# Laying plain row blocks between the four steps of a seven-product pair, in an encoder layer

## The chip, the core and the metric

The kernel runs on one core of a Trainium2 chip. The metric is the device time of one execution in microseconds; where several runs are shown, their median counts. Beside the runs there is one profiled execution, from which every view below is taken. A core has five engines that work at the same time and wait for one another by semaphores: TensorE (PE in the profile; its weight loads are PEld), VectorE (DVE), ScalarE (ACT), GpSimd (POOL) and SyncE (SP), whose queue issues most of the DMAs here.

## The reference, cut to what matters

One encoder layer over 256 tokens of width 4096, all in float32:

```python
h = rms_norm(x, g_mix)
proj = h @ w_in            # q latent, kv latent, rotary key, gate a | q_b, k_b, v_b, gate b
y_a = rms_norm(mla(...)) * silu(gate_a)
y_b = rms_norm(dilated(q_b, k_b, v_b)) * silu(gate_b)
x = x + concat(y_a, y_b) @ w_out
x = x + (p @ w_ple) * sigmoid(rms_norm(x, g_ple) @ w_ple_gate)
return rms_norm(x, g_final)
```

Nearly all of the arithmetic is in the three large products: with w_in (4096 x 11840), w_out and w_ple_gate (4096 x 4096 each).

## The kernel before, in words

**Products.** Every float32 operand is split into a high half (the value rounded to a shorter float, made by ScalarE: `split`, L115) and a low half (the rest, by VectorE: L116). A product of two tiles is then three matmuls into the same PSUM bank: high by high (L133), low weight by high (L134), high weight by low (L135). "Low" of L134 is that of the streamed weights, so L134 is the first matmul that needs VectorE's part of a conversion. The names of the tiles are `raw` for what a DMA brings, `hi` and `lo` for the halves; when a conversion goes to another place in memory, the name of that place stands instead (`B`, `T`, `Ah`, `Al` and so on).

**Row blocks.** The reduction over 4096 runs over 32 row blocks of 128. A load (L793) brings 128 rows of 1024 columns of the weights, 512 KB, into one of four `raw` tiles (`RAW = 4`). The 256 tokens are two halves of 128, the 1024 columns two halves of 512, so a row block that is done plainly takes four products (`plain_step`, one step).

**Seven-product blocks.** A block (`class Block`, L763 on) is 1024 output columns over all 32 row blocks. Some row blocks are taken in pairs: 2x2 halves of tokens and rows against 2x2 halves of rows and columns, done with seven products in place of eight. Such a pair is four steps (`fast_steps`), here called s1 to s4:

- s1 loads both row blocks; VectorE makes two differences (T[0]) and the low half of one half-width tile; 1 product
- s2 converts the second row block (high half L830, low half L833), and VectorE makes two more differences (T[1]; all differences are recorded at L817); 2 products
- s3 converts T[0], s4 converts T[1]; 2 products each

The differences and sums on the side of the tokens are made once, ahead of the block, by `add_sums`. T has one buffer. After the last step of the last pair a task forms the middle sums (`gates_mid`, `d_mid` with L669 and L672, `out_mid` with L904, `wide_mid`), which frees four of the eight PSUM banks; after the last step of the block another adds the rest (`d_done` with L687, `out_done` with L924 and the transposes of L730, `wide_done`).

There are 13 such blocks, 86 pairs in all: ga (part of gate a); q0, k0, v0, q1, k1, v1 (the dilated branch); three of w_out (called o0 to o2 here) and three of w_ple_gate. The rest of the columns goes through plain steps of two row blocks by 512 columns (`Old`).

**Order.** The program is written out by hand. `steps` is the list of all steps, and PE runs them in this order. How a block's pairs and plain row blocks follow one another was a string: in "CCSCSC..." a C is two plain steps and an S the four steps of a pair (`mix`, L1155; `lay`, L1161). k0, v0, q1 and k1 have "CSCSCSCSCSCSCSSC", eight pairs of which the last two stand back to back; the w_out block o1 and two of w_ple_gate end in "SSCC" and "SSCeC" (e: two steps with w_ple).

**Rings.** The converted tiles of a step lie in a ring: three `wp` tiles, and, in a block, further places that are idle at that time (`ring`). The main loop converts up to five steps ahead of the step that PE gets next, three more than otherwise (two), if the step's ring has more than three places; `tiles` gives no tile while its last user hasn't run (in the order of the program). All conversions stand in the in-order queues of ScalarE and VectorE together with the tasks above, in the order in which the program emits them. In k1 the last four letters (`spare = 4`) had the three `wp` tiles alone, because their fourth place, B4, becomes the result's.

Of the kernel before, what the change touches and what calls it, by code (L numbers as in the profile page):

```python
# [15 lines left out]
ALU = mybir.AluOpType  # L16
# [3 lines left out]
S = 256  # L20
# [58 lines left out]
def encoder_layer(ctx: ExitStack, tc: tile.TileContext, x, p, positions, g_mix, w_in, g_q_latent, w_uq,  # L79
                  g_kv_latent, w_ukv, g_out_mla, g_out_dil, w_out, w_ple, g_ple, w_ple_gate, g_final,  # L80
                  c_inv, c_dist, out):
    nc = tc.nc
    x, p, out = x[0], p[0, 0], out[0]
    w_in, w_uq, w_ukv, w_out, w_ple, w_ple_gate = (w[0] for w in (w_in, w_uq, w_ukv, w_out, w_ple, w_ple_gate))
# [24 lines left out]
    def plain(t):  # L109
        return t.bitcast(F32)  # L110
# [194 lines left out]
    T7 = {}  # L305

    sums = stat(NT * 6).rearrange("p (c t) -> p c t", t=NT)
# [162 lines left out]
    pairs = {}  # L470
# [182 lines left out]
    def d_mid(key, blk):  # L653
        def task():
            tags = D_TAGS[key]
            if len(tags) == 2:
                d = [slot(b, [NT, 512]) for b in tags]
            else:
                both = slot(tags[0], [2, NT, 512])
                d = [both[:, 0], both[:, 1]]  # L660
            D[key] = d
            if key == ("v", 1):
                E["d"] = slot("T5", [2, NT, S])
                nc.gpsimd.dma_start(E["d"], c_dist)
            ps = blk.ps
            sc = [(rxq if key[0] == "q" else rx)[:, t:t + 1] for t in range(NT)]

            def add(h, t, m, old):
                nc.vector.scalar_tensor_tensor(d[h][:, t], ps[m], sc[t], old, op0=ALU.mult, op1=ALU.add)  # L669

            for t in range(NT):
                nc.scalar.activation(d[0][:, t], ps["M1"], AF.Copy, scale=sc[t])  # L672
            for t in range(NT):
                add(1, t, "M6", d[0][:, t])
            add(0, 1, "M7", d[1][:, 1])
            add(1, 0, "M5", d[1][:, 0])
            add(1, 1, "M5", d[0][:, 1])
            flags.add(("mid", key))
            yield
        return task  # L680
# [71 lines left out]
    WP = ["wp"] * 3  # L752

    class Step:
# [4 lines left out]
        def __init__(self, load, split, run, needs=(), frees=0):  # L759
            self.load, self.split, self.run, self.needs, self.frees, self.after = load, split, run, needs, frees, None  # L760
            self.ring = WP
# [3 lines left out]
    class Block:  # L765
# [6 lines left out]

        NAMES = "M2", "X", "M3", "M4", "M1", "M5", "M6", "M7"

        def __init__(self, w, lhs, sums, name, order, needs, tags, tmp, ring, spare=0):
            self.w, self.lhs, self.sums, self.name, self.needs, self.tmp = w, lhs, sums, name, needs, tmp
            self.spare = spare
            self.ring, self.tags = ring, dict(zip(self.NAMES, tags))
            self.ps, self.left = {}, {}
            for kind, _ in order:  # L780
                for m in ("M1", "M5", "M7", "M6", "M4", "M2", "M3") if kind == "fast" else ("M2", "X", "M3", "M4"):
                    self.left[m] = self.left.get(m, 0) + (1 if kind == "fast" else 2)

        def product(self, m, a, b):
            first = m not in self.ps
# [23 lines left out]
        def fast_steps(self, j):  # L809

            r, T = [], []
            (A11, A21), (A12, A22) = [[lambda k=k, t=t: tuple(q[:, t * P:(t + 1) * P] for q in self.lhs(k))
                                       for t in range(NT)] for k in (2 * j, 2 * j + 1)]
            S = lambda n: (lambda: self.sums[j][n])

            def sub(dst, a, b):
                nc.vector.tensor_tensor(dst, a, b, op=ALU.subtract)  # L817

            def split1(hi, lo):
                if isinstance(self.tmp, tuple):  # L820
                    T.extend(slot(b, [2, Q]) for b in self.tmp)
                else:
                    both = slot(self.tmp, [4, Q])
                    T.extend((both[:, :2], both[:, 2:]))
                sub(T[0][:, 0], r[0][:, 1], r[0][:, 0])
                sub(T[0][:, 1], r[0][:, 1], r[1][:, 1])
                split(hi[:, 0], lo[:, 0], r[0][:, 0])

            def split2(hi, lo):
                nc.scalar.activation(hi, r[1], AF.Copy)  # L830
                sub(T[1][:, 0], r[1][:, 1], T[0][:, 0])
                sub(T[1][:, 1], r[1][:, 0], T[1][:, 0])
                nc.vector.tensor_tensor(lo, r[1], plain(hi), op=ALU.subtract)  # L833

            def run(*which):
                def go(hi, lo):
                    for i, (m, a) in enumerate(which):
                        self.product(m, a(), (hi[:, i], lo[:, i]))
                return go

            needs = [*self.needs(2 * j), *self.needs(2 * j + 1), (self.name, j)]
            return [
                Step(tuple(lambda k=k: r.append(self.load(k)) for k in (2 * j, 2 * j + 1)), split1, run(("M1", A11)), needs, 1),
                Step(None, split2, run(("M2", A12), ("M3", S(3))), needs, 1),
                Step(None, lambda hi, lo: split(hi, lo, T[0]), run(("M5", S(0)), ("M7", S(2))), needs, 0),
                Step(None, lambda hi, lo: split(hi, lo, T[1]), run(("M6", S(1)), ("M4", A22)), needs, 0),
            ]
# [304 lines left out]
    EVEN, ODD = ("m0", "m1", "s", "o", "m2", "m3", "t0", "t1"), ("m2", "m3", "t0", "t1", "m0", "m1", "s", "o")  # L1152
    LAST = "m2", "m3", "s", "o", "m0", "m1", "t0", "t1"

    def mix(shape, pairs=range(16)):  # L1155

        chosen = list(pairs)[:shape.count("S")]
        fast, plain_ = iter(chosen), iter(j for j in range(16) if j not in chosen)
        return [("ple", 0) if x == "e" else ("fast", next(fast)) if x == "S" else ("plain", next(plain_)) for x in shape]

    def lay(blk, order, mid, done, ple=None):  # L1161
        last = max(i for i, o in enumerate(order) if o[0] == "fast")
        for i, (kind, j) in enumerate(order):
            if kind == "fast":
                new = blk.fast_steps(j)
            elif kind == "ple":
                new = ple
            else:
                new = [x for kt in (2 * j, 2 * j + 1) for x in blk.plain_step(kt)]
            if i == last:  # L1170
                new[-1].after = mid
            if i == len(order) - 1:
                new[-1].after = done
            for x in new:
                x.ring = blk.ring if i < len(order) - blk.spare else WP
            steps.extend(new)

    def hook(at, f):
        assert at not in hooks
# [19 lines left out]

    hook(24, lambda: spawn(add_sums(7, x_pair, z0_dst, ("T2", "T3"), "x0_sums", x0_s, 2)))  # L1200
    gated_rings = {("T4", "T7"): ("mid", ("k", 1)), "Al1": ("y_sums", FAST_O - 1), ("T5", "T6"): "kpe"}
    order = mix("CCSCSCSCSCSCSCSC")
    blk = Block(w_in[:, OFF_GA:OFF_GA + 1024], lhs_x, x0_s, "x0_sums", order, lambda kt: (), LAST, ("T2", "T3"),
                WP + [("T5", "T6")])
    lay(blk, order, gates_mid(blk), gates_done(blk))
# [13 lines left out]
    x_s = {}  # L1219
# [10 lines left out]

    for n, key in enumerate((key, i) for i in range(2) for key in "qkv"):
        off = {"q": OFF_Q, "k": OFF_K, "v": OFF_V}[key[0]] + 1024 * key[1]
        full = "CSCSCSCSCSCSCSSC"
        order = mix("CCCCCCCCSCSCSCSC") if n == 0 else mix(full) if n < 5 else mix("CCCCSCSCSCSCSCSC", (0, 1, 2, 3, 6, 7))
        ring = (["B6"], ["B4", "B6"], ["B4", "B6"], ["B4"], ["B4"], [("T4", "T7")])[n]
        tags = LAST if n == 0 else ("t0", "t1", "m2", "m3", "m0", "m1", "s", "o") if n == 1 else (EVEN, ODD)[n % 2]
        blk = Block(w_in[:, off:off + 1024], lhs_x, x_s, "x_sums", order, lambda kt: (), tags, "B1", WP + ring,
                    4 if n == 4 else 0)
        lay(blk, order, d_mid(key, blk), d_done(key, blk))
    beside = [len(steps), len(steps) + 64]  # L1240
    for c in range(4):
        if c == 3:
# [5 lines left out]
    for k in range(WIDE_O):  # L1248
        hook(len(steps), only(*(("t0", "t1"), ("m0", "m1"), ("m2", "m3"))[k]))
        for h in range(2):  # L1250
            hook(len(steps) + 4 + h, lambda c=2 * k + h: load_res(c))
        order = mix(("CCCCCCSCSCSCSCCC", "CCSCSCSCSCSCSSCC", "CCCSCSCSCSCSCSCC")[k])
        blk = Block(w_out[:, 1024 * k:1024 * (k + 1)], lhs_y, y_s, "y_sums", order, lambda kt: need_y(kt // 2),
                    (EVEN, ODD)[k % 2], "Al2" if k < 2 else "Al1", WP + (["Ah2", "Al1"] if k < 2 else [("B7b", "T7")]))
        lay(blk, order, out_mid(k, blk), out_done(k, blk))
# [11 lines left out]
                     lambda j: ["pT"])  # L1267

    for k in range(WIDE):
        order = mix("CCCSCSCSCSCSCSCeC" if k == 0 else "CCSCSCSCSCSCSSCeC")  # L1270
        blk = Block(w_ple_gate[:, 1024 * k:1024 * (k + 1)], lhs_x1, x1_s, "x1_sums", [o for o in order if o[0] != "ple"],
                    lambda kt: [("x1T", kt // 4)], LAST, "B6", WP + ["B4"])
        lay(blk, order, wide_mid(k, blk), wide_done(k, blk), wide_ple(k))
    wide_end = len(steps)
# [221 lines left out]
```

## Time and profile before

| what | value |
|---|---|
| runs | 1947.1, 1948.03, 1950.61 us; median 1948.03 |
| the profiled execution | 1950.29 us |
| its span, first to last instruction | 1948.4 us |
| mean granted clock of TensorE | 0.996 |
| busy, share of the span | PE 98%, PEld 84%, DVE 80%, ACT 57%, POOL 4% |
| matmuls | 9275 |
| read from HBM | 364.72 MB, mean 189 GB/s |

A row of a group of instructions has the line, the engine, the operation, the tile it writes and those it reads (out<-in), then shapes. A row of waits has the waiting instruction, what released it, the sum in us, how often, and the longest. A row of the timeline has the start in us, the duration (of all, where several are merged, "x2"), and in brackets the idle time before it with what ended it. A row of a stretch has the busy time of each engine, the granted clock (PEclk), the share of the DMA engines' time and the rate.

### The profile page before, as it was taken

What the parts mean: (1) busy time and instruction counts of PE and PEld (TensorE: products, weight loads), DVE (VectorE), ACT (ScalarE), POOL (GpSimd) and SP (SyncE); (2) the same over time, 40 slices, a digit from 0 to 9 for tenths busy, and PEclk for the clock granted to TensorE, in tenths of its full rate; (3) what the DMA queues carried; (4) which work ended last, traced back from release to release, by engine and by line L of the source; (5) the groups of instructions that cost most, each with busy time, mean ns of one, the idle gap of its engine ahead of it and who ended that gap; (6) DMA issues with size and microseconds to landing.
All of it is one profiled execution on the core that took longest, in us unless ns stands there. A gap on an engine that the chain in (4) does not pass through costs nothing.

```text
span 1948.4 us, 25587 instructions
## 1 busy us (share of the span) xinstructions
PE 1916.1 (98%) x9275; PEld 1628.2 (84%) x9275; DVE 1556.9 (80%) x2167; ACT 1102.7 (57%) x1511; POOL 71.5 (4%) x124
## 2 busy tenths in 40 slices
PE   9999999999999999999999999999999999999997
PEld 8998889998888888887888888888888878888787
DVE  7767866665989989898787778988886688989765
ACT  6555565555555555655556666655555455656543
POOL 1001011110000000000000010000000000000000
PEclk9999999999999999999999999999999999999998
DMA  7666655455656666665664456665666656566665
GB/s 249 190 185 189 197 169 152 141 152 153 194 176 213 204 211 191 201 205 186 207 203 135 138 163 217 196 214 182 207 213 214 186 181 209 191 203 219 209 186 178
DMA packets 146478, 370.59 MB, mean 190 GB/s; under 512 B 11924, under 2 KB 45808, under 8 KB 146096
## 3 DMA queue, kind: packets, MB, share of 16 engines
q1 hardware_dynamic: 144432, 361.80, 60.1%
q0 software_dynamic: 1920, 7.15, 1.0%
q8 instruction: 73, 1.20, 0.3%
q14 instruction: 53, 0.43, 0.1%
HBM read 364.72 MB, written 4.19 MB: 189 GB/s over the span
## 4 chain that ended last, share of the span: by engine, by line
PE 83%; DVE 11%; issue 2%; DMA 2%; ACT 1%; SPq 0%; DVEq 0%; ACTq 0%
PE m L134 18%; PE m L135 18%; PE m L133 18%; PE o L134 3%; PE o L135 3%; PE o L133 3%; PE s L134 3%; DVE lo L116 3%; PE s L133 3%; PE s L135 3%; PE t L134 3%; PE t L135 3%; PE t L133 3%; DVE B L817 2%; DVE B L116 1%
## 5 line engine op out<-in xcount | busy, mean ns | idle before, releaser
L116 DVE TENSOR_TENSOR lo<-raw,hi 128x1024 fp32r<-128x1024 f32 (+3 forms) x507 | 557.8, 1108 | 206.1 <-ACT hi L115 205.7
L115 ACT ACTIVATE hi<-raw 128x1024 fp32r<-128x1024 f32 (+3 forms) x507 | 485.6, 965 | 290.2 <-PE m L135 152.5
L134 PE MATMUL m<-lo,Ah 128*128 128x512 f32 (+2 forms) x1133 | 426.5, 376 | 8.4 <-DVE lo L833 6.1
L133 PE MATMUL m<-hi,Ah 128*128 128x512 f32 (+2 forms) x1133 | 430.4, 380 | 1.3 <-ACT Al L115 0.8
L135 PE MATMUL m<-hi,Al 128*128 128x512 f32 (+2 forms) x1131 | 423.5, 374 | 0.0
L134 PEld LDWEIGHTS m<-lo,Ah 128*128 128x128 f32 x1133 | 213.4, 188 | 44.5 <-DVE lo L833 9.0
L135 PEld LDWEIGHTS m<-hi,Al 128*128 128x128 f32 x1131 | 212.8, 188 | 32.7 <-DVE Al L127 0.2
L133 PEld LDWEIGHTS m<-hi,Ah 128*128 128x128 f32 x1133 | 213.3, 188 | 31.9 <-ACT Ah L115 1.2
L115 ACT ACTIVATE hi<-B 128x1024 fp32r<-128x1024 f32 x90 | 95.4, 1061 | 122.6 <-PE o L135 65.6
L133 PE MATMUL m<-hi,B 128*128 128x512 f32 (+1 forms) x425 | 163.0, 384 | 0.0
L135 PE MATMUL m<-hi,B 128*128 128x512 f32 (+1 forms) x425 | 159.2, 375 | 0.0
L134 PE MATMUL m<-lo,B 128*128 128x512 f32 (+1 forms) x425 | 159.2, 375 | 0.0
L116 DVE TENSOR_TENSOR lo<-B,hi 128x1024 fp32r<-128x1024 f32 x90 | 108.6, 1221 | 34.6 <-ACT hi L115 34.6
L830 ACT ACTIVATE hi<-raw 128x1024 fp32r<-128x1024 f32 x57 | 60.6, 1064 | 55.4 <-PE o L135 30.4
L135 PEld LDWEIGHTS m<-hi,B 128*128 128x128 f32 x425 | 80.1, 189 | 12.1
L134 PEld LDWEIGHTS m<-lo,B 128*128 128x128 f32 x425 | 80.4, 189 | 11.1 <-DVE lo L116 0.2
L133 PEld LDWEIGHTS m<-hi,B 128*128 128x128 f32 x425 | 80.2, 189 | 10.8
L817 DVE TENSOR_TENSOR B<-raw,B 128x512 f32<-128x512 f32 x124 | 85.5, 689 | 2.2
L116 DVE TENSOR_TENSOR T<-t,T 128x512 fp32r<-128x512 f32 (+1 forms) x65 | 44.5, 685 | 41.7 <-ACT T L115 41.5
L116 DVE TENSOR_TENSOR B<-raw,B 128x1024 fp32r<-128x1024 f32 (+1 forms) x58 | 63.6, 1101 | 10.7 <-ACT B L115 10.7
L833 DVE TENSOR_TENSOR lo<-raw,hi 128x1024 fp32r<-128x1024 f32 x57 | 69.5, 1219 | 3.0 <-ACT hi L830 3.0
L115 ACT ACTIVATE B<-raw 128x1024 fp32r<-128x1024 f32 (+1 forms) x58 | 55.4, 960 | 27.0 <-PE o L135 11.2
(792 smaller groups left out, 3719.1 us busy)
## 6 DMA issues: line engine op xcount, KB each, us to landing
raw<-in_w_in_dram SPq DMA_DIRECT2D x320, 512.0 KB, 3.8
raw<-in_w_out_dram SPq DMA_DIRECT2D x128, 512.0 KB, 4.5
raw<-in_w_ple_gate_dram SPq DMA_DIRECT2D x128, 512.0 KB, 4.5
raw<-in_w_in_dram SPq DMA_DIRECT2D x63, 400.0 KB, 3.6
raw<-in_w_uq_dram SPq DMA_DIRECT2D x32, 384.0 KB, 3.4
raw<-in_w_ukv_dram SPq DMA_DIRECT2D x16, 512.0 KB, 4.3
T<-in_x_dram SPq DMA_DIRECT2D x7, 512.0 KB, 6.0
T<-in_x_dram POOLq DMA_DIRECT2D x7, 512.0 KB, 6.8
```

Source lines behind the costliest of these rows:

```text
L115: nc.scalar.activation(hi, src, AF.Copy)
L116: nc.vector.tensor_tensor(lo, src, plain(hi), op=ALU.subtract)
L133: nc.tensor.matmul(ps, ah, bh, start=start, stop=False)
L134: nc.tensor.matmul(ps, ah, bl, start=False, stop=False)
L135: nc.tensor.matmul(ps, al, bh, start=False, stop=stop)
L817: nc.vector.tensor_tensor(dst, a, b, op=ALU.subtract)
L830: nc.scalar.activation(hi, r[1], AF.Copy)
L833: nc.vector.tensor_tensor(lo, r[1], plain(hi), op=ALU.subtract)
```

## The change

The number of pairs in every block, which row blocks they take, and all instructions of a step stay. Four things are different.

- `weave` takes the place of `mix`: it lays `lead` plain steps first and `trail` last, and spreads the others evenly over the pairs; one of them goes between s1 and s2 of each pair, the others ahead of the pair. So k0 is now "c c s1 c s2 s3 s4 c s1 c s2 s3 s4 s1 c s2 s3 s4 c s1 c ...": one and two plain steps to a pair by turns. With seven pairs it is 1, 1, 2, 1, 2, 1, 2; with six, 1, 2, 2, 1, 2, 2 (in v1, where only two plain steps lead, 2, 3, 3, 2, 3, 3); with four, 1, 2, 1, 2 in q0 and two each in o0.
- `lay` goes step by step. The places of k0, v0, q1 get more: k0 and v0 three beside `wp` (B4, B6, B0), q1 two (B4, B6); k1 keeps B4. After the last pair of v0, q1 and k1 the place that the middle sums write is left out (`after`). For k1 that leaves `wp` alone for the last two steps, where before it was the last twelve.
- Leads and trails move a little: ga's first pair begins after six plain steps instead of four, o0's after 13 instead of 12 and with four behind the last pair instead of six, v1's after three instead of eight.
- In s2 VectorE makes the low half before the second of the two differences, not after it.

```diff
             def split2(hi, lo):
                 nc.scalar.activation(hi, r[1], AF.Copy)
                 sub(T[1][:, 0], r[1][:, 1], T[0][:, 0])
+                nc.vector.tensor_tensor(lo, r[1], plain(hi), op=ALU.subtract)
                 sub(T[1][:, 1], r[1][:, 0], T[1][:, 0])
-                nc.vector.tensor_tensor(lo, r[1], plain(hi), op=ALU.subtract)
...
+    def weave(fast, lead, trail, e=0):
+        n = len(fast)
+        inner, out, given = 32 - 2 * n - lead - trail, "c" * lead, 0
+        for i in range(n):
+            k = inner * (i + 1) // n - given
+            given += k
+            out += "c" * (k - 1) + "s" + "c" * (k > 0) + "sss"
+        out += "c" * trail
...
+        for i, key in enumerate(shape):
+            x = next(step[key])
+            x.ring = WP + list(after) if after != () and i > last else blk.ring
             if i == last:
-                new[-1].after = mid
...
-    order = mix("CCSCSCSCSCSCSCSC")
+    order = weave(range(7), 6, 2)
...
-        full = "CSCSCSCSCSCSCSSC"
-        order = mix("CCCCCCCCSCSCSCSC") if n == 0 else mix(full) if n < 5 else mix("CCCCSCSCSCSCSCSC", (0, 1, 2, 3, 6, 7))
-        ring = (["B6"], ["B4", "B6"], ["B4", "B6"], ["B4"], ["B4"], [("T4", "T7")])[n]
+        order = weave((range(4), range(8), range(8), range(8), range(8), (0, 1, 2, 3, 6, 7))[n], 16 if n == 0 else 2, 2)
+        ring = (["B6"], ["B4", "B6", "B0"], ["B4", "B6", "B0"], ["B4", "B6"], ["B4"], [("T4", "T7")])[n]
+        after = ((), (), ["B4", "B6"], ["B4"], [], ())[n]
...
-        order = mix(("CCCCCCSCSCSCSCCC", "CCSCSCSCSCSCSSCC", "CCCSCSCSCSCSCSCC")[k])
+        order = weave(*((range(4), 12, 4), (range(7), 4, 4), (range(6), 6, 4))[k])
...
-        order = mix("CCCSCSCSCSCSCSCeC" if k == 0 else "CCSCSCSCSCSCSSCeC")
+        order = weave(*((range(6), 6, 4) if k == 0 else (range(7), 4, 4)), 2)
```

More of the change, by code (lines that the diff above doesn't have):

```diff
@@ L773, in encoder_layer, with __init__ @@
         NAMES = "M2", "X", "M3", "M4", "M1", "M5", "M6", "M7"
-        def __init__(self, w, lhs, sums, name, order, needs, tags, tmp, ring, spare=0):
+        def __init__(self, w, lhs, sums, name, order, needs, tags, tmp, ring):
             self.w, self.lhs, self.sums, self.name, self.needs, self.tmp = w, lhs, sums, name, needs, tmp
-            self.spare = spare
             self.ring, self.tags = ring, dict(zip(self.NAMES, tags))
             self.ps, self.left = {}, {}
-            for kind, _ in order:
+            for kind, _ in order[0]:
                 for m in ("M1", "M5", "M7", "M6", "M4", "M2", "M3") if kind == "fast" else ("M2", "X", "M3", "M4"):
-                    self.left[m] = self.left.get(m, 0) + (1 if kind == "fast" else 2)
+                    self.left[m] = self.left.get(m, 0) + 1
         def product(self, m, a, b):
@@ L1153, in encoder_layer, with lay @@
     LAST = "m2", "m3", "s", "o", "m0", "m1", "t0", "t1"
[L1155 to L1169, printed above, removed]
-            if i == last:
-                new[-1].after = mid
[L1172 to L1176, printed above, removed]
+    def weave(fast, lead, trail, e=0):
[6 more added lines that the diff above has]
+        out += "c" * trail
+        if e:
+            out = out[:len(out) - trail + e] + "ee" + out[len(out) - trail + e:]
+        rest = [kt for kt in range(32) if kt // 2 not in fast]
+        return [("fast", j) for j in fast] + [("plain", kt) for kt in rest], out
+    def lay(blk, order, mid, done, ple=None, after=()):
+        pairs, shape = order
+        step = {"s": iter([x for kind, j in pairs if kind == "fast" for x in blk.fast_steps(j)]),
+                "c": iter([x for kind, kt in pairs if kind == "plain" for x in blk.plain_step(kt)]), "e": iter(ple or ())}
+        last = shape.rindex("s")
+        for i, key in enumerate(shape):
+            x = next(step[key])
+            x.ring = WP + list(after) if after != () and i > last else blk.ring
+            if i == last:
+                x.after = mid
+            if i == len(shape) - 1:
+                x.after = done
+            steps.append(x)
     def hook(at, f):
@@ L1232, in encoder_layer @@
         off = {"q": OFF_Q, "k": OFF_K, "v": OFF_V}[key[0]] + 1024 * key[1]
-        full = "CSCSCSCSCSCSCSSC"
-        order = mix("CCCCCCCCSCSCSCSC") if n == 0 else mix(full) if n < 5 else mix("CCCCSCSCSCSCSCSC", (0, 1, 2, 3, 6, 7))
-        ring = (["B6"], ["B4", "B6"], ["B4", "B6"], ["B4"], ["B4"], [("T4", "T7")])[n]
+        order = weave((range(4), range(8), range(8), range(8), range(8), (0, 1, 2, 3, 6, 7))[n], 16 if n == 0 else 2, 2)
+        ring = (["B6"], ["B4", "B6", "B0"], ["B4", "B6", "B0"], ["B4", "B6"], ["B4"], [("T4", "T7")])[n]
+        after = ((), (), ["B4", "B6"], ["B4"], [], ())[n]
         tags = LAST if n == 0 else ("t0", "t1", "m2", "m3", "m0", "m1", "s", "o") if n == 1 else (EVEN, ODD)[n % 2]
-        blk = Block(w_in[:, off:off + 1024], lhs_x, x_s, "x_sums", order, lambda kt: (), tags, "B1", WP + ring,
-                    4 if n == 4 else 0)
-        lay(blk, order, d_mid(key, blk), d_done(key, blk))
+        blk = Block(w_in[:, off:off + 1024], lhs_x, x_s, "x_sums", order, lambda kt: (), tags, "B1", WP + ring)
+        lay(blk, order, d_mid(key, blk), d_done(key, blk), after=after)
     beside = [len(steps), len(steps) + 64]
@@ L1269, in encoder_layer @@
     for k in range(WIDE):
-        order = mix("CCCSCSCSCSCSCSCeC" if k == 0 else "CCSCSCSCSCSCSSCeC")
-        blk = Block(w_ple_gate[:, 1024 * k:1024 * (k + 1)], lhs_x1, x1_s, "x1_sums", [o for o in order if o[0] != "ple"],
+        order = weave(*((range(6), 6, 4) if k == 0 else (range(7), 4, 4)), 2)
+        blk = Block(w_ple_gate[:, 1024 * k:1024 * (k + 1)], lhs_x1, x1_s, "x1_sums", order,
                     lambda kt: [("x1T", kt // 4)], LAST, "B6", WP + ["B4"])
```

## The prediction

> **What bounds the kernel now.** I read the page first, then the stretches block by block, then TensorE's own waits, and last the lines that those waits name. The page says who sets the end:
>
> ```profile
> span 1948.4 us, 25587 instructions
> ...
> PE 1916.1 (98%) x9275; PEld 1628.2 (84%) x9275; DVE 1556.9 (80%) x2167; ACT 1102.7 (57%) x1511; POOL 71.5 (4%) x124
> ...
> PE 83%; DVE 11%; issue 2%; DMA 2%; ACT 1%; SPq 0%; DVEq 0%; ACTq 0%
> ```
>
> TensorE (PE) is busy 98% of the span and carries 83% of the chain that ended last. The change takes away no matmul, so only time in which PE stands still, or runs slowly, can be won. How long PE needs is read from the starts of neighbouring matmuls in its timeline, because the printed ends are modelled and overlap:
>
> ```profile
> 1578.84 0.39 PE L135 MATMUL m<-hi,Al 128*128 128x512 f32 x1
> 1579.07 0.39 PE L133 MATMUL s<-hi,Ah 128*128 128x512 f32 x1
> ...
> 1583.83 0.39 PE L133 MATMUL m<-hi,Ah 128*128 128x512 f32 x1
> 1586.18 0.50 PE L134 MATMUL m<-lo,Ah 128*128 128x512 f32 x1 [1.96 <-DVE lo L833]
> ```
>
> A matmul starts every 0.227 us. A product is three of them, 0.68 us; a plain step has four products (2.72 us), a pair's four steps s1 to s4 have 1, 2, 2, 2 (0.68 and three times 1.36, together 4.76 us). The third and fourth rows show the loss that this change is about: in s2 the second matmul starts 2.35 us after the first, 2.12 us late, and waits for VectorE's L833, the low half of the pair's second row block. The printed idle time is 1.96, since the modelled end runs 0.16 past the next start (0.39 against 0.227); I add 0.16 to each printed wait.
>
> Two blocks side by side show how much a layout can cost (columns: stretch, length, busy time of PE, PEld, DVE, ACT, POOL, granted clock, DMA share, GB/s):
>
> ```profile
> 919.00:1002.00 83.00, 83.00 (x368) 68.78 (x367) 68.13 (x76) 43.27 (x45) 0.57 (x1) 1.00 0.66 211
> 832.00:919.00 87.00, 82.79 (x361) 66.97 (x360) 77.89 (x92) 47.75 (x50) 0.00 (x0) 1.00 0.61 192
> ```
>
> The first is v1 (six pairs, never two in a row), 122 products or 83.0 us: nothing lost. The second is k1 (eight pairs, the last two back to back): 120 products are 81.6 us, it takes 87. Its DVE is busy 90% of the stretch, so pairs fill DVE almost as fully as PE.
>
> **What PE waits for.** For L833 the view of that line, for the others TensorE's waits over the whole span (total us, times, longest):
>
> ```profile
>   PE m L134: 8.8, 8
> ...
>   PE t L134: 0.8, 1
> ```
>
> ```profile
> PE m L134 <- DVE lo L116: 2.3, 6, 1.3
> ...
> PE t L133 <- DVE T L116: 1.3, 1, 1.3
> PE m L730 <- DVE T L924: 1.2, 1, 1.2
> ...
> PE m L133 <- ACT Al L115: 0.8, 1, 0.8
> ...
> PE t L134 <- DVE lo L116: 0.3, 1, 0.3
> ```
>
> And two stretches right behind the longest waits run at a lower granted clock:
>
> ```profile
> 1586.00:1591.00 5.00, 4.82 (x14) 3.85 (x15) 4.83 (x12) 2.58 (x4) 0.00 (x0) 0.66 0.37 109
> 1816.00:1823.00 7.00, 5.42 (x16) 3.76 (x15) 6.76 (x8) 4.69 (x6) 0.00 (x0) 0.76 0.49 157
> ```
>
> So the blocks lose: (A) to L833, 8.8 + 0.8 in 9 waits, with 0.16 each 11.0 us; (B) to the clock, 5 x 0.34 + 7 x 0.24 = 3.4 us; (C) to the other five rows, 5.9 in 10 waits, 7.5 us. Together **21.9 us**, which is the most that this change can win from what these rows show.
>
> **The change part by part.** Instructions, loads and products stay the same in number; three things move.
>
> *The subtraction.* For a pair's steps on DVE:
>
> ```profile
> 956.87 0.69 DVE L116 TENSOR_TENSOR lo<-raw,hi 128x512 fp32r<-128x512 f32 x1
> 957.48 1.42 DVE L817 TENSOR_TENSOR B<-raw,B 128x512 f32<-128x512 f32 x2
> ...
> 963.61 2.35 DVE L116 TENSOR_TENSOR lo<-raw,hi 128x1024 fp32r<-128x1024 f32 x2
> 965.87 0.69 DVE L817 TENSOR_TENSOR B<-raw 128x512 f32<-128x512 f32 x1
> ```
>
> By starts, a half-width subtraction or low half takes 0.60 us and a full low half 1.13 (965.87 less 963.61, halved). L833 now stands behind one L817 instead of two and ends 0.60 us sooner, if its high half is there. It is: ScalarE made it
>
> ```profile
> 955.88 1.06 ACT L830 ACTIVATE hi<-raw 128x1024 fp32r<-128x1024 f32 x1 [0.73 <-PE t L135]
> ```
>
> by 956.94, before the first of the two subtractions even began. Only where PE has no need yet does L833 wait for ScalarE now, 3.0 us in four places (the line's view):
>
> ```profile
>   ACT hi L830: 3.0, 4
> ```
>
> There DVE would idle 0.6 longer, 2.4 us in all that PE doesn't see. The subtraction behind it feeds s4, whose high half (1.06 on ACT) lies beside s3's low half (1.13 on DVE): nothing.
>
> *The plain step between s1 and s2.* It gives PE 2.72 us more to do before s2 and DVE 1.13 more: 1.59 us relief. With the moved subtraction 2.19, over the longest wait of 2.12: all nine waits of (A) go. What is late next is s3, which has the 1.59 but not the 0.60: its shortage is that of s2 plus 1.13 less 1.36, less 1.59, so 0.3 us where s2 lacked 2.12 and nothing elsewhere. (B) goes with the waits ahead of it.
>
> *Even layout.* Two pairs back to back cost DVE 2 x 6.4 (four subtractions and a short low half at 0.60, three at 1.13) against PE's 9.5. Now each pair has at least one plain step: 7.5 on DVE against 7.5 on PE; every second or third has two, 8.7 against 10.2. That is balance, not surplus, for 38 pairs with one step (I count them from the layout rule), and no more than two of those follow each other.
>
> Of (C), the waits in k1's tail come partly from something that stays. There the middle sums stand on DVE ahead of the last plain step's low half:
>
> ```profile
> 911.63 2.19 DVE L669 SCALAR_TENSOR_TENSOR B<-t,st,B 128x512 f32<-128x512 f32 x3
> 913.74 1.40 DVE L669 SCALAR_TENSOR_TENSOR B<-m,st,B 128x512 f32<-128x512 f32 x2
> 915.06 2.35 DVE L116 TENSOR_TENSOR lo<-raw,hi 128x1024 fp32r<-128x1024 f32 x2
> ```
>
> These five sums need 3.4 us from s4's first product on (0.68), then the low half 1.13: 5.2 us after s4 begins, with some 0.3 for signals 5.5, against 1.36 + 2.72 + 0.23 = 4.3 until PE asks. k1's last two steps still have only three tiles, so the last one is converted behind the sums, and I keep 1.5 us there. In the other blocks a fourth tile puts that conversion ahead of the sums. Of L730's 1.4 I keep half: its DVE work sits in the queue behind row blocks that landed late after two pairs back to back. The rest of (C) goes: T L116 (ga's first pair starts two steps later, its s3 three) and Al (one more plain step ahead).
>
> *Rings.* More tiles let k0, v0 and q1 convert one step further ahead; PE's waits there are already counted. The new tiles are idle until the middle sums, which come after the last pair. Cost nothing; the cover is the 2 plain steps behind that pair (5.4 us).
>
> *Loads, the unknown.* Each plain step carries a 512 KB load on SP's queue, past which it moves too. A load waits for the raw tile four loads back. A pair's second raw tile is now released after the laid-between step, and where one plain step separates pairs, the next such step's load waits for that release.
>
> ```profile
> raw<-in_w_in_dram SPq DMA_DIRECT2D x320, 512.0 KB, 3.8
> ...
> raw<-in_w_ple_gate_dram SPq DMA_DIRECT2D x128, 512.0 KB, 4.5
> ```
>
> With four tiles, PE frees s2's tile s4 + s1 + plain + s2 = 6.1 us before the next plain step's; s2's conversion takes 1.06 + 1.13 of it, so 3.9 us are left for 3.8 or 4.5 of landing. A landing up to 0.6 late is covered: the tile comes free s3 + s4 + s1 = 3.4 us before PE's use, the conversion needs 2.2, and the low half is asked for 0.2 later, 1.4 spare. The ends are 0 and, if a landing takes the 6.0 us of the chain's longest piece in o1's tail,
>
> ```profile
> 1382.37 6.02 DMA raw<-in_w_out_dram
> ```
>
> 0.7 us for each of 38 pairs, 27 us. The medians of 576 loads are nearer to 0; I take **2 us**.
>
> Sum: 21.9 - 0.3 - 1.5 - 0.7 = 19.4 won, 2 lost, **17.4 us**. The profiled execution took 1950.3 us (1.9 around its span), 2.3 over the median of 1948.0 of the runs shown; the waits are differences, so I take them off the median: 1930.6, say **1931**.
>
> **Rivals.** *Clock.* [...] As a mechanism of this kernel: the drops are tied to their place, not to the waits, and 3.4 us stay, 1934. The rows put both drops straight behind the waits of about 2 us, so I give it 0.06.
> *Loads a little late.* 0.3 us per one-step pair, 11 us, 1940: for it, DMA is busy 0.6 to 0.66 and the margin is negative without the spare; against it, v1 lost nothing at 211 GB/s. 0.14.
> *Only the subtraction works*, because DVE balance uses up what the plain step gives: of (A) 0.60 goes from seven waits and 0.32 from two, 4.8 us, with or without (B): 1940 to 1943. 0.07.
> *Slower: loads 6 us or longer.* From a landing of 5.3 us on (3.9 + 1.4), each one-step pair waits for the rest; at 6.0 that is 27 us against 19.4 won, 1956. The point where it turns to slower is 5.8 us. For it: one such piece; against it: the medians. 0.08.
> *New waits just eat the gain*, 1944 to 1952: 0.03.
>
> **How the numbers follow.** My forecast, 1924 to 1936 by itself, has 0.62: its low end has all of 21.9 won with 2 us of scatter between runs, its high end the loads at 7 us. The range 1924 to 1942 adds the clock rival, the late loads and about half of the subtraction rival: 0.85. About 0.2% (3.9 us) is what a measurement here can tell from no change. Faster by more: 0.62 + 0.06 + 0.14 + 0.07 = 0.89, less 0.02 for scatter, 0.87; the same 0.04, slower 0.09.
>
> **What would show it.** Right: PE's waits for the line of L833 fall from 9.6 to under 1 us; k1 takes about 83.5 us and the last block of ple_gate loses its 0.76; the clock stays at 1.00 there; one wait near 1 us stays at k1's last step. Wrong: waits of ScalarE on raw loads grow from place to place in the one-step pairs and PE waits on low halves of plain steps (loads); s3 or s4 become the waiting steps (DVE); a clock drop without a wait before it (clock).

## The result, and the profile after

The changed kernel takes 1934.64 us (median of 4 runs, 1934.4 to 1935.21) against 1947.9 (median of 4, 1947.1 to 1950.61): 13.3 us less, a ratio of 0.993 with a 95% interval of 0.9913 to 0.9947. Between the two profiled executions, which the working of the prediction was made against, it is 15.7 us: 1934.55 against 1950.29. The prediction was 1931, 17.4 us less, in a range of 1924 to 1942.

The page of the changed kernel, in the places that were shown of before: PE carries 91% of the chain that ended last (83% before), DVE 5% (11% before).

```profile
span 1932.6 us, 25589 instructions
...
PE 1910.8 (99%) x9275; PEld 1625.3 (84%) x9275; DVE 1559.3 (81%) x2167; ACT 1100.6 (57%) x1511; POOL 71.5 (4%) x124
...
PE 91%; DVE 5%; DMA 1%; ACT 1%; issue 1%; SPq 0%; DVEq 0%; ACTq 0%
```

In the changed file the low half of a pair's second row block has the line L831 (L833 before). The view of that line, part "who waited for it", no longer has a row of PE; all that is left is one weight load:

```profile
who waited for it (us, times):
  PEld m L134: 0.3, 1
```

So the nine waits of 9.6 us are gone. What PE waits for in the changed kernel, over the whole span, in rows of 0.5 us and more (who waits for whom, then total us, times, longest):

```profile
PE m L134 <- DVE lo L116: 2.9, 7, 1.2
PE m L1435 <- DVE junk L1429: 1.5, 1, 1.5
PE t L270 <- DMA T<-in_x_dram: 0.9, 1, 0.9
PE m L134 <- DVE B L116: 0.9, 2, 0.6
PE o L133 <- ACT T L115: 0.7, 1, 0.7
PE m L133 <- ACT Ah L125: 0.7, 1, 0.7
PE m L134 <- DVE T L116: 0.6, 1, 0.6
PE m L730 <- DVE T L923: 0.5, 1, 0.5
```

L1435, L270, the row of L125 and the one with o belong to the start, the end and the attention, outside the blocks. Four rows are left for the blocks: 2.9 + 0.9 + 0.6 + 0.5 = 4.9 us in 11 waits, or 6.7 with the 0.16 that the prediction adds to each, where 21.9 us stood before (the clock's 3.4 included). That is 15.2 us won, and the profiled executions differ by 15.7.

The stretch of k1 and the two places where the clock had dropped, at the same times in the changed kernel:

```profile
826.00:910.00 84.00, 82.82 (x365) 68.26 (x364) 78.75 (x92) 48.57 (x50) 0.00 (x0) 1.00 0.64 200
1584.00:1591.00 7.00, 7.00 (x33) 5.79 (x32) 6.86 (x9) 3.92 (x5) 0.00 (x0) 1.00 0.64 219
1816.00:1823.00 7.00, 7.00 (x33) 5.79 (x32) 3.05 (x3) 4.63 (x7) 0.00 (x0) 1.00 0.85 278
```

PEclk is 1.00 in all. The 84 us of the first row hold a little more than k1: 365 matmuls, 82.7 us at 0.227 each. From its first matmul to that of the next block k1 takes 83.1 us, where 83.5 were predicted; before, the same 360 matmuls took 87.3. The 9275 matmuls and POOL's 71.5 us are the same.

### The profile page after: what moved, and what is told of

It is laid out like the page before. It is cut to its first block, busy times and chain, and to the rows that moved or that the text cites. A ratio compares the mean times of both kernels' runs of the same rounds, so it can differ in the third digit from the quotient of the medians.

```text
span 1932.6 us, 25589 instructions
## 1 busy us (share of the span) xinstructions
PE 1910.8 (99%) x9275; PEld 1625.3 (84%) x9275; DVE 1559.3 (81%) x2167; ACT 1100.6 (57%) x1511; POOL 71.5 (4%) x124
## 4 chain that ended last, share of the span: by engine, by line
PE 91%; DVE 5%; DMA 1%; ACT 1%; issue 1%; SPq 0%; DVEq 0%; ACTq 0%
PE m L134 20%; PE m L135 19%; PE m L133 19%; PE t L134 4%; PE t L135 4%; PE t L133 4%; PE o L134 3%; PE o L135 3%; PE o L133 3%; PE s L134 3%; PE s L135 3%; PE s L133 3%; DVE lo L116 1%; DMA raw<-in_w_ple_gate_dram 1%; PE t L443 1%
## 5 line engine op out<-in xcount | busy, mean ns | idle before, releaser
L116 DVE TENSOR_TENSOR lo<-raw,hi 128x1024 fp32r<-128x1024 f32 (+4 forms) x506 | 559.7, 1110 | 231.0 <-ACT hi L115 227.6
L115 ACT ACTIVATE hi<-raw 128x1024 fp32r<-128x1024 f32 (+4 forms) x506 | 486.9, 967 | 368.0 <-PE m L135 142.6
L133 PE MATMUL m<-hi,B 128*128 128x512 f32 (+1 forms) x417 | 159.3, 382 | 0.0
L135 PE MATMUL m<-hi,B 128*128 128x512 f32 (+1 forms) x417 | 155.6, 373 | 0.0
L115 ACT ACTIVATE hi<-B 128x1024 fp32r<-128x1024 f32 x71 | 75.1, 1060 | 72.2 <-DVE B L816 35.3
L116 DVE TENSOR_TENSOR lo<-B,hi 128x1024 fp32r<-128x1024 f32 x71 | 86.3, 1222 | 3.7 <-ACT hi L115 1.5
L115 ACT ACTIVATE B<-B 128x1024 fp32r<-128x1024 f32 (+1 forms) x63 | 60.7, 963 | 46.3 <-DVE B L816 25.0
L831 DVE TENSOR_TENSOR lo<-raw,hi 128x1024 fp32r<-128x1024 f32 x61 | 74.3, 1219 | 1.7 <-ACT hi L829 1.7
```

The source lines that it names most:

```text
L115: nc.scalar.activation(hi, src, AF.Copy)
L116: nc.vector.tensor_tensor(lo, src, plain(hi), op=ALU.subtract)
L133: nc.tensor.matmul(ps, ah, bh, start=start, stop=False)
L135: nc.tensor.matmul(ps, al, bh, start=False, stop=stop)
```

## The experiments

Twelve kernels were run. Where a run was timed beside the kernel before, that kernel's median in the same set is given, since it moves by a microsecond or two from set to set.

**The subtraction alone (e1).** The kernel before with `split2` of the changed one:

```diff
                 sub(T[1][:, 0], r[1][:, 1], T[0][:, 0])
+                nc.vector.tensor_tensor(lo, r[1], plain(hi), op=ALU.subtract)
                 sub(T[1][:, 1], r[1][:, 0], T[1][:, 0])
-                nc.vector.tensor_tensor(lo, r[1], plain(hi), op=ALU.subtract)
```

> The kernel before with only the subtraction moved. My theory: each of the nine waits of PE on the second step's low half shrinks by 0.60 us (two of 0.32 vanish), 4.8 us in all, and one or both clock drops behind the two longest waits go; the waits of k1's tail and of the transposes at the start of o2 stay. 1940 to 1943.5 us. Rival, the subtraction is most of the gain and the layout little: 1936 to 1938, with no PE wait on that line left. Rival, the drops are tied to their place: 4.8 us and no more, with both stretches still below a clock of 0.8.

1944.54 us against 1948.46 (ratio 0.9981, 0.9972 to 0.9989): 3.9 us, a little less than expected (1940 to 1943.5). The view of its line (L832 here):

```profile
  PE m L134: 4.3, 6
  PEld t L134: 0.5, 1
```

9.6 us in 9 waits became 4.3 in 6. So the mechanism is as predicted, and each remaining wait fell by about 0.7. Neither clock drop is in this trace (mean granted clock 0.998, against 0.996 in that of before), though waits of 1.4 and 0.8 us stay at the same two places: the drops are not tied to the place alone. The rest of the gain is left to the layout.

**Layout and rings without the subtraction (e2).** The changed kernel with the old `split2`.

> The changed kernel with the subtraction back in its old place: layout and rings alone. My theory: the plain step laid between s1 and s2 gives 1.59 us relief, which is more than eight of the nine waits; only the longest (2.12) leaves 0.5 us, and s2 in the tight places may wait a little: 1935 to 1936.5 us. Rival, the subtraction's 0.60 us are needed in many places: 1938 to 1940, with PE waits on the line of s2's low half over 3 us in all.

1935.37 us against 1948.46 (0.9934, 0.992 to 0.9947). One wait on the line of s2's low half is left (0.6 us), in gate a and not where the longest had been. The 0.7 us of e1 isn't additive: once the layout stands, the moved subtraction is worth less than 1 us, at the edge of what these runs can tell.

**Even spacing, whole pairs (e3).** All plain steps ahead of their pair:

```diff
-            out += "c" * (k - 1) + "s" + "c" * (k > 0) + "sss"
+            out += "c" * k + "ssss"
```

> The changed kernel with the same even spacing, but all plain steps ahead of a pair and none between s1 and s2. My theory: no two pairs stand back to back, so the waits at the ends of blocks go; at the starts of blocks s2 has only the 0.60 of the subtraction, so waits of 0.3 at k0, 0.7 at k1 and 1.5 at the first block of ple_gate come back: 1937 to 1939 us. Rival, even spacing is all that counts: 1934 to 1935.5. Rival, the place between s1 and s2 is all that counts: 1941 or more.

1933.76 us against 1948.46 (0.9926, 0.9913 to 0.9938). My theory fell here. Between s1 and s2 or ahead of s1, the plain step stands ahead of s2 in both, and so it gives the same relief; the waits that I expected back at the starts of k0, k1 and the first w_ple_gate block stayed away; one of 0.8 us stands in gate a. e3 is no slower than the changed kernel.

**The rings of before (e4).**

```diff
-        ring = (["B6"], ["B4", "B6", "B0"], ["B4", "B6", "B0"], ["B4", "B6"], ["B4"], [("T4", "T7")])[n]
-        after = ((), (), ["B4", "B6"], ["B4"], [], ())[n]
+        ring = (["B6"], ["B4", "B6"], ["B4", "B6"], ["B4"], ["B4"], [("T4", "T7")])[n]
+        after = ()
...
+        if n == 4:
+            for late in steps[-12:]:
+                late.ring = WP
```

> The changed kernel with the rings of before (k0 and v0 two places beside wp, q1 one, k1 one and none in its last twelve steps). My theory: once pairs aren't back to back, four or five tiles are enough, and three just so: 1934.5 to 1936 us, a wait of up to 1.5 us at k1's end. Rival, the further places carry part of the gain: 1938 or more, with PE waits inside k0, v0, q1 and k1 of over 3 us in all.

1934.57 us against 1948.46 (0.993, 0.9918 to 0.9943), the changed kernel's time. So the added places carry nothing that these runs can tell, with the step between and the moved subtraction in place.

**Even spacing without the other two (e5).** e3 with the old `split2`; the rings and the moved leads and trails of the changed kernel stay.

> Even spacing with whole pairs, and the subtraction in its old place: neither the step between s1 and s2 nor the moved subtraction, rings as changed. My theory now: what counts is how much work of TensorE stands ahead of s2, not where; with a plain step ahead of every pair s2 has at least 2.72 us more than in two pairs back to back and at a block's start, so the subtraction's 0.7 us matter only where VectorE is behind anyway (gate a, the first w_ple_gate block): 1934 to 1936 us, blocks lose 10 to 12 us in all. Rival, whole pairs need the subtraction: 1937 to 1940, with waits on s2's low half of over 4 us in all.

1935.08 us against 1949.52 (0.9929, 0.9916 to 0.9941), 14.4 us less. The view of s2's line in the whole list of PE's waits:

```profile
PE m L134 <- DVE lo L832: 2.1, 2, 1.5
...
PE m L134 <- DVE B L832: 1.1, 2, 0.6
```

Four waits, 3.2 us, at gate a and early in the three w_ple_gate blocks, where VectorE is behind with tasks from before. No wait is left in the dilated blocks on this line. In all, the blocks lose 7.4 us in 9 waits (6.0 printed), less than the 10 to 12 expected. So the spacing, with the extra plain step ahead of the first s2 and no two pairs back to back, makes nearly the whole gain. What the moved leads and trails do in it was not run by itself.

**Three raw tiles (e6).** `RAW, AHEAD = 3, 2`. This prices the loads.

> The changed kernel with three raw tiles instead of four: it prices the loads. My theory: a load then waits for the tile three back, so a pair's second load can start only when the s2 before it is converted; conversion to conversion that is a landing of 3.8 to 4.5 us plus 4.7 us on VectorE, against 7.5 us of TensorE in a one-step pair: 1 to 1.7 us late in each of 38 pairs that nothing hides: 1970 to 2000 us, and the other pairs hardly. Rival, the loads have ample room and four tiles aren't near their limit: under 1940.

2080.46 us (two runs) against 1949.52: 131 us slower than the kernel before and 146 slower than the changed one. The direction is as expected and the size is not: 146 us over 86 pairs is 1.7 us for each pair, not for the 38 one-step pairs alone. Of it, some 15 us are the clock's, an estimate from the mean granted clocks of the two traces: 0.990 over 2077.6 us here, 0.997 over 1932.6 in the changed kernel's (20.8 less 5.8). PE now waits for conversions in nearly every pair, and ScalarE's conversions for raw loads (the last row; 39.1 in 24 in the changed kernel):

```profile
PE m L134 <- DVE lo L116: 37.1, 56, 1.2
PE m L133 <- ACT hi L115: 17.4, 28, 2.0
PE m L134 <- DVE B L116: 9.1, 11, 1.4
PE m L133 <- ACT B L115: 6.8, 6, 1.6
```

```profile
ACT hi L115 <- DMA raw<-in_w_in_dram: 131.1, 50, 5.8
```

Three raw tiles are thus too few. The trace shows where the loss stands: set beside the changed kernel's, matmul by matmul, k0 to k1 lose 46 us, and 43 of them at the plain step between s1 and s2. The median two-step pair there loses 1.6 us, the median one-step pair 0.7. So the theory had the wrong pairs and the wrong step; why the two-step pairs pay more was not run.

**Slack first, and k1's end (e7, e8).** e7 lays the two-step pairs ahead of the one-step pairs and turns k1's ring; e8 is the same with whole pairs.

```diff
-            k = inner * (i + 1) // n - given
+            k = -(-inner * (i + 1) // n) - given
...
-                    lambda kt: (), tags, "B1", WP + ring)
+                    lambda kt: (), tags, "B1", ring + WP if n == 4 else WP + ring)
```

> The changed kernel with the two-step pairs first (2, 1, 2, 1 for 1, 2, 1, 2; 2, 1, 2, 1, 2, 1, 1 for seven) and, in k1, the fourth place taking the first turn of the ring instead of the last, so that the last plain step finds a free wp tile one step sooner and is converted ahead of the middle sums. My theory: k1's last wait of 1.34 us goes; the waits early in gate a and in the w_ple_gate blocks, where VectorE has tasks from before, shrink by half, 1 to 2 us: 1931 to 1932.5 us. Rival, the early waits come from the load of the two-step pairs themselves and the end of the blocks suffers: 1933.5 or more.

1934.04 us against 1949.52 (0.9923, 0.9909 to 0.9936), above the 1931 to 1932.5 expected.

> As the run before, with whole pairs (no plain step between s1 and s2). My theory: as with the other spacing, the place within the pair is worth nothing: 1930.5 to 1932.5 us. Rival, the step between is worth its 1.6 us once the rest is gone: over 1 us slower than the run before.

1932.73 us against 1949.52 (0.9918, 0.9904 to 0.9931), 0.2 us above what was expected and no slower than e7. In both, k1's wait only moved. PE's waits in e7 from 820 to 912 us:

```profile
PE m L133 <- ACT B L115: 1.1, 1, 1.1
PE m L134 <- DVE B L116: 0.8, 1, 0.8
```

They stand at k1's first step, whose tile is now B4, which q1's last step still holds. The gain of the early slack was eaten by this, and in e7 by waits late in the last w_ple_gate block (at 1783 and 1800 us), which e8 doesn't have.

**k1's end again (e9).** The turns of the rings of q1 and k1 are put so that both of k1's last steps find a free `wp` tile.

```diff
-... ["B4", "B6"], ["B4"], [("T4", "T7")])[n]
-        after = ((), (), ["B4", "B6"], ["B4"], [], ())[n]
+... ["B6", "B4"], ["B4"], [("T4", "T7")])[n]
+        after = ((), (), ["B4", "B6"], [], [], ())[n]
...
-                    lambda kt: (), tags, "B1", WP + ring)
+                    lambda kt: (), tags, "B1",
+                    ring + WP if n == 3 else ["wp", "wp", "B4", "wp"] if n == 4 else WP + ring)
```

> The changed kernel with the turns of the rings of q1 and k1 put so that k1's last plain step finds a free wp tile one step sooner; in VectorE's order its low half then stands ahead of the five middle sums and not behind them. My theory: PE's wait of 1.3 us at k1's last step goes, nothing comes at k1's start: the thirteen blocks lose 1.3 us less, 1933 to 1933.7 us. Rival, as in the run before where the wait only moved to k1's first step: 1934.3 or more, with a wait of over 1 us at one end of k1.

1932.17 us against 1949.35 (0.991, 0.9896 to 0.9923), a little below the 1933 to 1933.7 expected. Its trace has no PE wait between 820 and 912 us, where the changed kernel has this one:

```profile
PE m L134 <- DVE lo L116: 1.2, 1, 1.2
```

The wait of L730 went too, with the new turns of the rings; that wasn't meant, and why is open.

**The mix (e10).** e9 with, in gate a, the two-step pairs first, and in w_ple_gate whole pairs with the two-step pairs first.

> The run before with, in gate a, the two-step pairs first (pairs split), and in the three w_ple_gate blocks whole pairs with the two-step pairs first. My theory: gate a's waits fall from 3.0 to 1.2 us, those of w_ple_gate from 5.2 to about 1, since a pair's second raw tile is free one plain step sooner there and its loads land in time: 1928 to 1930.5 us. Rival, the waits in w_ple_gate come from VectorE's tasks and not from loads: 1931 or more.

1926.15 us against 1949.35 (0.9878, 0.9864 to 0.9891), below the 1928 to 1930.5 expected, the best of all and 8.5 us below the changed kernel. All that PE waits for in the blocks is 0.4 us:

```profile
span 1925.0 us, 25581 instructions
...
PE 1907.5 (99%) x9275; PEld 1626.2 (84%) x9275; DVE 1557.8 (81%) x2167; ACT 1100.7 (57%) x1511; POOL 71.5 (4%) x124
```

```profile
PE m L134 <- DVE lo L116: 0.4, 2, 0.2
```

**What of the mix did it (e11, e12).** Each puts one thing back in the w_ple_gate blocks: e11 the plain step between s1 and s2, e12 the one-step pairs first.

> The mix with one thing put back: in the three w_ple_gate blocks a plain step stands between s1 and s2 again (the two-step pairs stay first). My theory: there the second raw tile is held one plain step longer and loads take longest, so ScalarE waits on raw loads more and 2 to 4 us of PE waits come back: 1928 to 1930. Rival, the order of the two-step pairs is what helped: 1926 to 1927.

1929.91 us against 1948.09 (0.9905, 0.9891 to 0.992).

> The mix with the other thing put back: in the three w_ple_gate blocks the one-step pairs stand first again (pairs whole). My theory: VectorE still has the tasks of the block before there, so the first block's and the early waits of the others come back, 2 to 3 us: 1928 to 1929.5. Rival, whole pairs alone did it: 1926 to 1927.

1929.3 us against 1948.09 (0.9902, 0.9885 to 0.9918). They take 3.8 and 3.2 us more than the mix, in another set, whose kernel before was 1.3 us faster; both theories said so, and neither alone did it. The traces tell them apart: in e12 the waits stand early in each of the three blocks, where VectorE still has tasks of the block before; in e11 they stand late in the last block, from about 1778 us on, in plain steps. By the starts of neighbouring matmuls these waits make 3.0 us in e11 and 2.0 in e12, against 0.5 in the mix, so in e12 about half of the difference between the medians. The same place of the changed kernel shows what is late. VectorE and then PE:

```profile
1779.83 0.69 DVE L816 TENSOR_TENSOR B<-raw,raw 128x512 f32<-128x512 f32 x1 [1.63 <-DMA raw<-in_w_ple_gate_dram]
```

```profile
1783.53 0.50 PE L134 MATMUL m<-B,Ah 128*128 128x512 f32 x1 [0.63 <-DVE B L116]
```

And the DMAs of the changed kernel, first those issued from 1771.5 to 1774 us, then those from 1746 to 1830 (KB each, median us to landing):

```profile
raw<-in_w_ple_gate_dram SPq DMA_DIRECT2D x2, 512.0 KB, 7.7
```

```profile
raw<-in_w_ple_gate_dram SPq DMA_DIRECT2D x28, 512.0 KB, 4.7
B<-in_g_final_dram POOLq DMA_DIRECT2D x2, 1024.0 KB, 8.1
```

Two loads took 7.7 us instead of 4.7. They were issued just when POOL's queue began to fetch the final gain, 1 MB at a time (its first issue stands at 1771.42 us). It is not the only such place: all nine raw loads of the changed kernel that took over 6.5 us (after 150 us) were issued while a load of POOL's queue was under way, near 1166, 1368, 1466, 1771 and 1791 us. No run moved those fetches, so that they are the cause is read from these times and not tried. In the mix the final gain is fetched beside raw loads too (9.3 us for one fetch; the median of the five raw loads issued from 1765 to 1776 us is 5.3), and PE hardly waits; by the order of the steps, whole pairs have their second raw tile free one plain step sooner.

## Why the prediction was right, and where its terms were off

**(A), the waits on s2's low half.** Right: nine waits, 9.6 us, gone. The relief was put together from two parts, the step between s1 and s2 and the subtraction. e5 shows that neither is needed for most of it: one more plain step ahead of s2, also ahead of s1, is enough. e1 shows that the subtraction alone takes 5.3 us of 9.6, about 0.7 from a wait that remains and not 0.60. In the trace of before L833 began at 958.81, 1.33 us after the first subtraction in the row of 957.48; behind one subtraction it begins 0.60 after it. The second difference reads the first and starts 0.73 behind it (1.42 for the two, of 0.69 each), where the prediction had 0.60 for every one.

**(B), the clock.** The drops went, but 3.4 us was the wrong size against the median. The profiled execution of before had both drops and stood 2.4 us above the median of its four runs. In the fifteen runs of before beside e1 to e4, those with a mean granted clock of 0.998 took 1946.5 to 1947.9 us and those at 0.995 or 0.996 took 1948.9 to 1952.1: by these clocks a drop comes in some executions and not in others. Nine of the fifteen are at 0.997 or 0.998, like the trace of the changed kernel (0.997), in which the clock stays at 1.00 while the products run. Taking a loss that one execution shows off a median of runs that mostly lack it was the step that failed: "the waits are differences, so I take them off the median" holds for waits that are in every run. It accounts for 2.4 of the 4.1 us between the forecast and the result.
The clock rival, that the drops hang on their place and stay, is not borne out: they stood behind waits of 2.1 and 1.7 us, and with the waits gone the clock is 1.00 at both places and the four runs of the changed kernel are at 0.997 or 0.998, within 0.8 us of one another.

In the profiled execution of before the clock goes to 0.50 at 1586.87 and at 1818.97, for 3.41 us each. Matmuls start 0.43 us apart there, against 0.227; by the clock each drop costs 3.41 x 0.50 = 1.7 us, an estimate. Another wait of 1.7 us, in k1, had no drop. The 3.41 us ahead of the first drop, the first drop, the 3.41 us ahead of the second, and those up to the end of k1's wait, in the columns of the stretches above:

```profile
1583.46:1586.87 3.41, 1.45 (x7) 0.90 (x6) 3.27 (x9) 1.77 (x2) 0.00 (x0) 1.00 0.51 154
1586.87:1590.28 3.41, 3.41 (x10) 2.63 (x9) 3.31 (x7) 1.29 (x2) 0.00 (x0) 0.50 0.51 154
...
1815.56:1818.97 3.41, 1.83 (x8) 0.88 (x6) 3.38 (x6) 2.76 (x4) 0.00 (x0) 1.00 0.45 138
...
904.51:907.92 3.41, 1.88 (x7) 0.89 (x6) 3.38 (x6) 2.52 (x3) 0.00 (x0) 1.00 0.42 118
```

By the starts of its matmuls, PE stood still 2.2 us in the first, 2.0 in the third and 2.0 in the last. So here as much standing still had a drop behind it at one place and none at another, and what decides it is not shown.

**(C), the rest.** k1's last wait was kept at 1.5 and measured 1.2 printed, 1.34 by starts; e9 shows its cause, the place of the last low half behind the middle sums. The 0.3 us for signals in the working of that 1.5 was the author's estimate; the changed kernel shows 0.4. The first sum begins at 902.66, 0.50 us after the last matmul that it waits for (902.16), so 0.27 beyond that matmul's 0.227, and PE goes on at 907.35, 1.26 after the low half began (906.09), so 0.13 beyond its 1.13. Half of L730's wait was kept, and 0.5 printed of 1.2 stayed. That was luck: in e3 and e5, which set no two pairs back to back either, 1.2 and 1.1 stay, so the reason given for the half doesn't carry, and what sets this wait is open. Gate a failed: the wait of 1.3 on T went, but others took its place.

```profile
PE m L134 <- DVE T L116: 0.6, 1, 0.6
PE m L134 <- DVE lo L116: 0.5, 1, 0.5
```

The layout puts two one-step pairs first there, while VectorE still works through the chains of small instructions that belong to the latents. The even spacing counts only the blocks' own work; with the slack first, 0.2 us of this is left in the mix.

**Even spacing.** Right that two pairs back to back were the cause at the ends of q1, k1 and two w_ple_gate blocks (e5, where no s2 waits there), and that one-step pairs are balanced: in the changed kernel none of the sixteen one-step pairs of k0 to k1 waits.

**Rings.** Costed at nothing and worth nothing (e4).

**Loads.** 2 us were taken, and the last block's wait of 0.8 is all that the trace shows of them. One of the prediction's own signs of being wrong came in part: ScalarE's waits on raw loads rose from 47.1 us (the sum of all such rows; the largest was 13.3 in 7) to 114.9:

```profile
ACT hi L115 <- DMA raw<-in_w_in_dram: 39.1, 24, 4.5
ACT hi L115 <- DMA raw<-in_w_ple_gate_dram: 21.0, 13, 3.3
ACT B L115 <- DMA raw<-in_w_in_dram: 20.4, 8, 4.4
ACT hi L115 <- DMA raw<-in_w_out_dram: 18.4, 11, 2.7
```

PE feels it in one place only, the last block, at a two-step pair. The slower rival put the loss at one-step pairs whose laid-between load takes over 5.3 us. The changed kernel has 27 one-step pairs that follow another pair directly; their loads took 3.5 to 5.6 us, two of them over 5.3, and PE didn't wait at either. So its condition was hardly met, and e6, which takes a raw tile away, is no test of it.

**Sum.** Predicted to stay or come in the blocks: 0.3 + 1.5 + 0.7 + 2 = 4.5 us. Measured: 6.7, or 7.0 by the starts of neighbouring matmuls. Of the 7.0, k1's end has 1.3, L730 0.8 and the last block's load 0.8. Gate a has 1.8 and the early waits of the w_ple_gate blocks 2.3, for which the prediction set down next to nothing; VectorE is busy there (14.8 of 15 us from 1745 to 1760). These 4.1 were missed, and the 1.2 that the loads didn't take hid part of it.

## What to carry to other kernels

When a seven-product pair fills VectorE as fully as TensorE, spread the pairs evenly and never set two back to back; what counted in the dilated blocks is how much work of TensorE stands ahead of the step that waits, not its exact place, and the spare steps belong where other tasks still load VectorE. Before laying anything between the uses of a buffer, work out how much longer the buffer is held: by the prediction's working the raw tiles here had about one microsecond of spare, and two late loads used it up. And set a loss that the profile of one execution shows against the runs' scatter before it is taken off their median.

## What was not expected of the hardware

- Raw tiles have a cliff: four cost nothing that the trace shows outside the last block, three cost 146 us (2080.46 against 1934.64), in k0 to k1 43 of 46 us at the step laid between s1 and s2.
- In the profiled execution of before the granted clock fell to 0.50 twice, for 3.41 us each, behind waits of 2.1 and 1.7 us; behind a wait of 1.7 us in k1 it stayed at 1.00. The fifteen runs of before beside e1 to e4 lie up to 5.5 us apart (1946.5 to 1952.1), with mean clocks from 0.998 to 0.995.
- Beside one 1 MB fetch on POOL's queue, two 512 KB loads on SP's queue took 7.7 us to land, against a median of 4.7 in that block.
